# Two DMA rings, two halves of the rows: a row-wise roll with a narrower SBUF part

## The chip, the cores and the metric

The kernel runs on one core of one Trainium2 chip. A core has compute engines (TensorE, VectorE or DVE, ScalarE or ACT, GpSimd or POOL), a sequencer without arithmetic (SyncE or SP), and 16 DMA engines that move data between HBM and HBM, or between HBM and the on-chip memory SBUF. SP, ACT and POOL can issue DMAs, each into a queue of its own. The metric is device time in microseconds (us), lower is better.

## The reference

```python
def setup_inputs():
    return {
        "x": np.random.randn(8192, 8192).astype(np.float32),
        "shift": 100,
    }

def reference(x: np.ndarray, shift: int) -> np.ndarray:
    return np.roll(x, shift, axis=1)
```

Each row of 8192 floats (32 KB) is rotated to the right by 100 columns: output columns 100 to 8191 are input columns 0 to 8091, and output columns 0 to 99 are the last 100 of the input. Nothing is computed; 268.4 MB are read and 268.4 MB are written. The source and destination of one byte lie 400 B apart within a row, except for the 100 columns that wrap around.

## The kernel before

The shift `s` is 100. The kernel cuts each output row at a column `a`, which is `s` rounded up to a multiple of 128, and, by L21 and L22, 128 more: `a` is 256. `g = a - s` is 156.

**Columns `a` to the end** are copied from HBM to HBM by the two hardware queues ("rings"), SP's and ACT's. The rows are taken in blocks of 64 (`c`). Within a block, DMA `j` (0 to 3) has 16 rows, 4e + j for e from 0 to 15, which go one to each DMA engine; each is a contiguous run of 7936 floats (31,744 B). SP issues j = 0 and 2, ACT issues j = 1 and 3, of every block (L36 to L38). So each ring has 256 DMAs of 496 KB, both rings walk through the same blocks from row 0 to row 8191, and an engine's four rows of a block are neighbours in memory. Each queue issues in order, and from its fifth DMA on it waits for an older one to land before it issues another.

**Columns 0 to `a`** go through SBUF on POOL's queue, whose descriptors are written by software ("q0" in the profile). The rows are taken in `n_st` = 4 groups of P x J x Q = 128 x 4 x 4. For three of every four rows, one "lead" DMA reads a contiguous run of `a` floats that begins `s` floats before the row, and so takes in the end of the row above (L66 to L68, 12 DMAs into tile `t`). The run's first `s` floats belong to the output row above, and the rest to the row itself: two copies on VectorE put them into tile `h` (L70 and L73). The end of the fourth row and the beginning of the first are loaded straight into `h` (L69 and L72, 4 DMAs each). When all groups have been loaded, 16 DMAs write `h` to the output (L77), 1 KB to a row. The framework adds the semaphore waits between these; POOL's DMAs cycle through 8 semaphores, so that one is issued when the one eight before it has landed.

All three queues start at once and share the 16 DMA engines.

Of the kernel before, what the change touches and what calls it, by code (L numbers as in the profile page):

```python
# [1 line left out]

# [4 lines left out]


@with_exitstack
def kernel(  # L10
    ctx: ExitStack,
    tc: tile.TileContext,
    x: bass.AP,
    shift: int,
    out: bass.AP,
):
    nc = tc.nc
    n_rows, n_cols = x.shape
    s = shift % n_cols
    a = -(-s // 128) * 128  # L20
    if 0 < a <= 384 and a + 128 <= n_cols:  # L21
        a += 128  # L22
    g = a - s
    P = nc.NUM_PARTITIONS
    engines = [nc.sync, nc.scalar]
    n_chunks = 16
    rows = n_rows // n_chunks

    xm = x.rearrange("(c e j) w -> c j e w", e=16, j=4)
    om = out.rearrange("(c e j) w -> c j e w", e=16, j=4)
    if a < n_cols:
        for c in range(n_rows // 64):  # L36
            for j in range(4):
                engines[j % 2].dma_start(out=om[c, j, :, a:], in_=xm[c, j, :, g:n_cols - s])  # L38
    if a == 0:
        return  # L40


    if a > 512:
        for i in range(n_chunks):
            r = slice(i * rows, (i + 1) * rows)
            nc.gpsimd.dma_start(out=out[r, :s], in_=x[r, n_cols - s:])
            if g > 0:
                nc.gpsimd.dma_start(out=out[r, s:a], in_=x[r, :g])
        return

    Q, J = 4, 4
    n_st = n_rows // (P * Q * J)
    reads = ctx.enter_context(tc.tile_pool(name="reads", bufs=n_st))
    heads = ctx.enter_context(tc.tile_pool(name="heads", bufs=n_st))
    xt = x.rearrange("(k p j q) c -> k q p j c", q=Q, j=J, p=P)
    ot = out.rearrange("(k p j q) c -> k q p j c", q=Q, j=J, p=P)  # L60
    tiles = []
    for k in range(n_st):
        t = reads.tile([P, Q - 1, J, a], x.dtype)
        h = heads.tile([P, Q, J, a], x.dtype)
        for q in range(1, Q):
            lead = bass.AP(tensor=x.tensor, offset=(k * P * J * Q + q) * n_cols - s,  # L66
                           ap=[[J * Q * n_cols, P], [Q * n_cols, J], [1, a]])
            nc.gpsimd.dma_start(out=t[:, q - 1], in_=lead)  # L68
        nc.gpsimd.dma_start(out=h[:, Q - 1, :, :s], in_=xt[k, Q - 1, :, :, n_cols - s:])  # L69
        nc.vector.tensor_copy(h[:, :Q - 1, :, :s], t[:, :, :, :s])  # L70
        if g > 0:
            nc.gpsimd.dma_start(out=h[:, 0, :, s:], in_=xt[k, 0, :, :, :g])  # L72
            nc.vector.tensor_copy(h[:, 1:, :, s:], t[:, :, :, s:])  # L73
        tiles.append(h)
    for k, h in enumerate(tiles):
        for q in range(Q):
            nc.gpsimd.dma_start(out=ot[k, q, :, :, :a], in_=h[:, q])  # L77


# [1 line left out]
_INS = ['x', 'shift']  # L81
_OUTS = [((8192, 8192), 'float32')]

_NUMBERS = {'shift': 100}


# [26 lines left out]
```

## Time and profile before

| what | value |
|---|---|
| median of 6 runs | 819.53 us (819.27 to 821.43) |
| the profiled execution | 821.43 us, its span 819.3 us |
| busy: VectorE, POOL | 7.7 us, 28.8 us |
| DMA packets | 21,060, 276.89 MB, mean 338 GB/s |
| ring copies, issue to landing | 12.6 us (median, SP and ACT alike) |
| POOL's stores, issue to landing | 113.2 us (median) |
| POOL's last issue | 373.4 us after the span's start |

The span is the part of the execution that the profile covers. "GB/s" counts each transfer once, whether it reads HBM and writes HBM, or has SBUF at one end. A queue's share is the time that its packets were open on the 16 engines, as a part of 16 times the span; a packet that waits for memory is open too. q1 and q10 are the two rings, q0 is POOL's queue. Where a queue waits, the row names the waiting queue and line first, and then what it waited for.

### The profile page before, as it was taken

To read this page: it belongs to the slowest core of one execution; us is meant where nothing else is said; L and a number is where in the kernel's file an instruction comes from. 1 tells how busy PE (TensorE), PEld (TensorE's weight loads), DVE (VectorE), ACT (ScalarE), POOL (GpSimd) and SP (SyncE) were. 2 spreads that over 40 slices of the span, in tenths; PEclk is the share of its full clock that TensorE was granted. 3 is DMA by queue.
4 is the path that set the end of the run, shared out by engine and by line. 5 is a ranking of instruction groups with operands and counts; after the bars stand their busy time and mean duration, and the time that the engine had idled before them with its cause. 6 is when DMAs were issued, how large, how long until landed. Compare 5 with 4: busy or idle time off the path is not lost. (4 is left out here: it accounts for less than half of the span.)

```text
span 819.3 us, 617 instructions
## 1 busy us (share of the span) xinstructions
DVE 7.7 (1%) x8; POOL 28.8 (4%) x40
## 2 busy tenths in 40 slices
DVE  0000000000000000000000000000000000000000
POOL 3000000000010000000000000000000000000000
DMA  9999999999999999999999999999999999999997
GB/s 309 336 346 345 346 342 351 348 348 353 352 359 359 353 347 353 350 356 358 336 344 336 336 330 330 336 332 329 335 330 333 331 332 332 336 332 324 327 330 257
DMA packets 21060, 276.89 MB, mean 338 GB/s; under 512 B 8768, under 2 KB 8768, under 8 KB 12864
## 3 DMA queue, kind: packets, MB, share of 16 engines
q10 hardware_dynamic: 8192, 130.04, 46.2%
q1 hardware_dynamic: 8192, 130.04, 45.9%
q0 software_dynamic: 4672, 16.78, 6.9%
q14 instruction: 4, 0.03, 0.0%
HBM read 268.44 MB, written 268.44 MB: 655 GB/s over the span
## 5 line engine op out<-in xcount | busy, mean ns | idle before, releaser
L77 POOL DMA_DIRECT2D out_dram<-h x16 | 13.2, 825 | 198.6 <-DMA out_dram<-h 111.1
L68 POOL DMA_DIRECT2D t<-in_x_dram x12 | 9.5, 793 | 59.8 <-DMA h<-in_x_dram 30.2
L70 DVE COPY h<-t 128x1200 f32<-128x1200 f32 x4 | 3.1, 786 | 233.3 <-DMA t<-in_x_dram 233.3
L73 DVE COPY h<-t 128x1872 f32<-128x1872 f32 x4 | 4.9, 1225 | 0.0
L69 POOL DMA_DIRECT2D h<-in_x_dram x4 | 3.0, 748 | 44.8 <-DMA t<-in_x_dram 44.8
L72 POOL DMA_DIRECT2D h<-in_x_dram x4 | 3.0, 748 | 41.9 <-DMA t<-in_x_dram 41.9
L94 POOL MEMSET const-float32-0.0<- 128x1 f32 x1 | 0.1, 98 | 0.2 <-issue 0.2
L94 POOL MEMSET const-bfloat16-1.0<- 128x1 bf16 x1 | 0.1, 101 | 0.0
L94 POOL MEMSET const-float32-1.0<- 128x1 f32 x1 | 0.1, 98 | 0.0
L94 POOL MEMSET const-uint8-127<- 128x1 uint8 x1 | 0.1, 98 | 0.0
## 6 DMA issues: line engine op xcount, KB each, us to landing
out_dram<-in_x_dram SPq DMA_DIRECT2D x256, 496.0 KB, 12.6
out_dram<-in_x_dram ACTq DMA_DIRECT2D x256, 496.0 KB, 12.6
out_dram<-h POOLq DMA_DIRECT2D x16, 512.0 KB, 113.2
t<-in_x_dram POOLq DMA_DIRECT2D x12, 512.0 KB, 95.0
h<-in_x_dram POOLq DMA_DIRECT2D x4, 312.0 KB, 93.6
h<-in_x_dram POOLq DMA_DIRECT2D x4, 200.0 KB, 98.0
```

The source lines that it names most:

```text
L68: nc.gpsimd.dma_start(out=t[:, q - 1], in_=lead)
L69: nc.gpsimd.dma_start(out=h[:, Q - 1, :, :s], in_=xt[k, Q - 1, :, :, n_cols - s:])
L70: nc.vector.tensor_copy(h[:, :Q - 1, :, :s], t[:, :, :, :s])
L72: nc.gpsimd.dma_start(out=h[:, 0, :, s:], in_=xt[k, 0, :, :, :g])
L73: nc.vector.tensor_copy(h[:, 1:, :, s:], t[:, :, :, s:])
L77: nc.gpsimd.dma_start(out=ot[k, q, :, :, :a], in_=h[:, q])
L94: nc = _bacc.Bacc("TRN2", target_bir_lowering=False, num_devices=1)
```

## The change

`a` loses the extra 128 columns: it is 128, and `g` is 28. The rings' rows are 8064 floats (32,256 B). SP takes the blocks of the first half of the rows and ACT those of the second half, each of them all four `j` of a block; they are issued alternately in the program. `J` is 8, so that POOL's part has two groups of 128 x 8 x 4 rows: 6 lead DMAs and 2 + 2 straight loads, 4 copies, and 8 stores, with 512 B to a row.

```diff
     s = shift % n_cols
     a = -(-s // 128) * 128
-    if 0 < a <= 384 and a + 128 <= n_cols:
-        a += 128
     g = a - s
...
     if a < n_cols:
-        for c in range(n_rows // 64):
+        half = n_rows // 64 // 2
+        for c in range(half):
             for j in range(4):
-                engines[j % 2].dma_start(out=om[c, j, :, a:], in_=xm[c, j, :, g:n_cols - s])
+                for q, eng in enumerate(engines):
+                    eng.dma_start(out=om[q * half + c, j, :, a:], in_=xm[q * half + c, j, :, g:n_cols - s])
...
-    Q, J = 4, 4
+    Q, J = 4, 8
     n_st = n_rows // (P * Q * J)
```

## The prediction

> **What bounds the kernel now.** I read the page's slices and queues first, then the queue's own waits, then the DMA view of two stretches, one with and one without the GpSimd queue's traffic. Compute engines can be left at once: VectorE is busy 7.7 us and POOL 28.8 us of 819.3.
>
> The slices and the queues of the page:
>
> ```profile
> DMA  9999999999999999999999999999999999999997
> GB/s 309 336 346 345 346 342 351 348 348 353 352 359 359 353 347 353 350 356 358 336 344 336 336 330 330 336 332 329 335 330 333 331 332 332 336 332 324 327 330 257
> ...
> q10 hardware_dynamic: 8192, 130.04, 46.2%
> q1 hardware_dynamic: 8192, 130.04, 45.9%
> q0 software_dynamic: 4672, 16.78, 6.9%
> ...
> HBM read 268.44 MB, written 268.44 MB: 655 GB/s over the span
> ```
>
> The 16 DMA engines are busy from the first slice to the last (46.2 + 45.9 + 6.9 = 99.0% of their span). There is no gap to close: the time changes only if the engines have less to do or do it at another rate. The GB/s row, which counts each transfer once, falls from about 350 to about 331 in the middle, where the GpSimd queue (q0) runs dry. The two rings are not short of issues, as the waits of SP's queue show (who waited, for what, us in total, times, longest):
>
> ```profile
> SPq L38 <- DMA out_dram<-in_x_dram: 672.0, 252, 4.3
> ```
>
> 252 of SP's 256 issues stood ready and waited for an older transfer. Now the DMA view of 20 to 180 us, where q0 mostly loads, and then of 500 to 800 us, where it is empty (packets, MB, share of the 16 engines):
>
> ```profile
> q10 hardware_dynamic: 1553, 24.76, 43.1%
> q1 hardware_dynamic: 1546, 24.54, 41.3%
> q0 software_dynamic: 1706, 6.03, 16.1%
> ```
>
> ```profile
> q10 hardware_dynamic: 3129, 49.65, 50.1%
> q1 hardware_dynamic: 3130, 49.69, 49.4%
> ```
>
> What limits the engines is read from two rates. Per engine, the rings move 49.30 MB / (84.4% x 16 x 160 us) = 22.8 GB/s in the first stretch and 99.34 MB / (99.5% x 16 x 300 us) = 20.8 GB/s in the second: a row of 31,744 B takes 1,391 ns beside q0, and 1,526 ns without it. An engine doing a fixed job per byte would not change by 10%. HBM traffic does stay put: a ring's byte is read from HBM and written to it, a q0 byte touches HBM once, so the first stretch has (2 x 49.30 + 6.03) / 160 us = 654 GB/s and the second 2 x 99.34 / 300 us = 662. The same sum gives 659 for 180 to 260 us, 665 for 260 to 400 (mostly q0 stores) and 665 for 400 to 500. So HBM traffic is within 2% of constant while the engines' own rate moves by 10%: I read the bound as HBM, not the engines' count of bytes. (That every slice is 9 tells only that an engine always has a packet open, also one that waits for memory.)
>
> The page "HBM Reference", section Specifications, of the Trainium skill gives a domain about 716 GB/s; 536.9 MB at that would take 750 us by an estimate from that figure, so this run would stand at 91% of it, and a new order would have more to lose than to gain.
>
> **The change part by part.** The profiled execution took 821.43 us with a span of 819.3, 2.1 us outside it; the median of the runs is 819.53, 1.9 below the profiled one. I make the sum on the span and carry the difference over unchanged.
>
> *1. Narrower SBUF part (the two removed lines at L21; a is 128, not 256, and g 28, not 156).* HBM traffic is unchanged: each byte of x is read once and each of out written once, 536.9 MB, by either route. What moves is 8192 x 512 B = 4.19 MB from "load and store through q0" to "one ring copy": q0 falls from 16.78 to 8.39 MB, the rings rise from 260.08 to 264.27 MB, engine bytes in all fall from 276.86 to 272.66 MB. A ring row grows from 31,744 to 32,256 B, in the same 256 DMAs of 16 rows on SP and 256 on ACT.
> - HBM rate held: the stretches with q0 get half as long. Against 662 GB/s, 20 to 180 us lost 160 x 8/662 = 1.9 us, 180 to 260 lost 80 x 3/662 = 0.4, and 260 to 500 gained 240 x 3/662 = 1.1. Net 1.2 lost, half of it returned: about -0.6 us.
> - Durations of each stretch kept for ring bytes (22.8, 22.5, 21.6, 21.0 and 20.8 GB/s per engine from the five stretches named above): with the q0 stretches halved, the rings need 751 us of engine time where they needed 726, q0 27 where it needed 54, in the 780 us from 20 to 800: -2 us.
> - Lower end, flat per byte: 272.66/276.86 of the span, -12.4 us. Only if every engine byte cost the same, which the 10% above contradicts.
> - Upper end, q0 priced by the piece: there are as many contiguous pieces as before (loads 6,144 + 2,048 + 2,048, stores 8,192), only shorter. If they kept q0's whole 6.9% (56.5 us per engine), the added 4.19 MB on the rings at 333 GB/s would come on top: +12.6 us. Single packet records speak against it: in the first 170 us a load packet of four 1,024 B pieces took 281 ns on the mean (1,200 packets) and one of eleven 400 B pieces 343 ns (78 packets), 70 and 31 ns a piece. The packet's bytes set the price, and 8 x 512 B makes the same 4 KB packet.
>
> I take -0.7 us: the first of these, a tenth towards the second, because the HBM rate is the steadiest number of the trace.
>
> *2. J 8 instead of 4 (L55).* Two groups of rows instead of four. The program as built issues 18 DMAs on POOL, not 36, each of 1,024 pieces and up to 512 KB as before, and 4 copies on VectorE, not 8. The rows of before:
>
> ```profile
> L77 POOL DMA_DIRECT2D out_dram<-h x16 | 13.2, 825 | 198.6 <-DMA out_dram<-h 111.1
> L68 POOL DMA_DIRECT2D t<-in_x_dram x12 | 9.5, 793 | 59.8 <-DMA h<-in_x_dram 30.2
> L70 DVE COPY h<-t 128x1200 f32<-128x1200 f32 x4 | 3.1, 786 | 233.3 <-DMA t<-in_x_dram 233.3
> L73 DVE COPY h<-t 128x1872 f32<-128x1872 f32 x4 | 4.9, 1225 | 0.0
> ```
>
> Copies become 2,400 and 672 elements a partition, about 1.5 and 0.5 us each by these rows; POOL's issue time lies between half of 28.8 us (a price per DMA) and all of it (per piece). Neither is on the path: POOL's last issue is at 373 us and its last landing about 113 us later, 330 us before the end. Half the bytes bring that to some 250 us. Cost nothing; it would matter only if q0 outlived the rings. The first copy waits for a larger first group, and only the group's own stores wait behind it.
>
> *3. Halves (L35 to L38).* SP walks rows 0 to 4095, ACT rows 4096 to 8191, in the same blocks of 64 rows, one row per engine. Before, an engine took rows 4e, 4e+1, 4e+2, 4e+3 in turn from the two rings, 32 KB apart; now it alternates between two streams 128 MB apart, each going 32 KB a step. DMA count, rows per DMA, issue time (510 ns on SP, 517 on ACT, under 672 us of waiting) and each ring's bytes stay equal, so both still end together. What stands open is only how HBM takes two distant streams for one. No row shows this. The nearest are the slices that hold ring copies alone (500 us on, the last left out): they run from 324 to 336 GB/s about a mean of 331, with one program at different places of the tensors. That bounds it at +2.2% (+18 us) and -1.5% (-12 us). I take 0: the rate of slices 25 to 36 shows no trend as the rings walk through the second half of both tensors, and within a DMA the 16 rows stand to each other as before.
>
> A rule speaks against this part. The page "DMA: Bandwidth & Descriptors", section Latency and other measured facts, of the Trainium skill, row on HBM row pitch at large powers of two, has copies at a pitch of 512 KiB at 207 GB/s per direction, 2 MiB at 164, and 4 MiB at 103. If two streams a power of two apart collided so, ring time would grow by 207/164, an estimate of some 1,030 us; no run here shows it, and 16 rows 128 KB apart run at 331 here. As a sign it points to slower.
>
> Sum: 819.3 - 0.7 + 0 + 0 = 818.6 us of span, 820.7 for that execution, 818.8 against the median.
>
> **The rivals.** About 0.2% (1.6 us) is what a measurement of this kernel can tell from no change.
> - *A, no change:* HBM stays the bound at the same rate. 818.8, own range 816.5 to 820.5.
> - *B, slower: the two streams cost HBM time.* Place: each ring packet after q0 is done. Price: between 0.3% and the 2.2% of the slowest slice, so 821.3 to 837, middle 827. It decides when a ring row of 32,256 B takes over 1,526 x 32,256/31,744 x 1.003 = 1,555 ns in the q0-free stretch. For it: HBM is the bound, so any lost efficiency shows in full, over all 780 us, and two neighbouring rows become two distant ones. Against it: the rows inside each DMA keep their spacing.
> - *C, faster: engine bytes pay, or separate regions suit HBM.* -2 us by the durations, -12.4 flat: 807 to 817.5, middle 813. For it: the engines are at 99% and get 1.5% fewer bytes. Against it: the HBM sum.
> - *D, slower: 512 B pieces cost as much as 1 KB ones.* Up to +12.6: 821.5 to 832. Against it: the packet records.
> - *The change does not do what it says:* excluded for the transfers' shapes, since the built program has 256 DMAs of 16 x 8064 on each ring; if the rings drifted apart their regions would be as distant anyway.
>
> **How the numbers follow.** A 0.42, B 0.35, C 0.17, D 0.06. A is the likeliest single case and gives the predicted time. Of A, 0.10 falls under -0.2%, 0.28 within, 0.04 above. Faster 0.10 + 0.17 = 0.27; same 0.28; slower 0.04 + 0.35 + 0.06 = 0.45. Range 806 to 837: the lower end is the -12 of parts 1 and 3, not both at once, the upper the +18 of B; what is left out is gains that add up and the rule's large price, under 0.15 together.
>
> **What will show it.** Right: q0 at about 8.4 MB and 3.5 to 4% with its packets ending near 250 us; rings at 132.1 MB each and some 95.5% together; 331 GB/s in the q0-free slices, which begin earlier; an HBM rate of 654 to 656 over the span. B shows as q0-free slices under 330 GB/s with all slices still 9. C shows as those slices above 333. D shows as a q0 share near 6.9% at half the bytes. The prediction falls if q0-free slices move by more than 1%, whatever q0 does: then part 3 was mispriced at 0.

## The result and the profile after

The changed kernel takes 826.07 us (median of 20 runs, 822.11 to 828.87); the kernel before took 820.36 us (median of 42) beside it. The ratio is 1.0069, 95% interval 1.0059 to 1.0080: about 5.7 us slower. The profiled execution has a span of 823.9 us, 4.6 more than before.

The page of the kernel after, slices and queues:

```profile
DMA  9999999999999999999999999999999999999997
GB/s 312 337 340 341 337 347 344 352 356 346 336 347 326 329 332 327 330 327 334 329 334 324 337 324 335 324 324 332 323 337 330 330 321 330 337 327 326 327 326 262
...
q10 hardware_dynamic: 8192, 132.14, 47.8%
q1 hardware_dynamic: 8192, 132.14, 47.2%
q0 software_dynamic: 2336, 8.39, 3.9%
...
HBM read 268.44 MB, written 268.44 MB: 652 GB/s over the span
```

All slices but the last are still 9, so the engines nearly always have a packet open; q0's bytes have halved and its share nearly so; the drop in the GB/s row comes at slice 13 instead of slice 20. After the drop the row lies about 329, not 331. The queue's waits, and the DMA view of 500 to 800 us, in which the rings run alone in both kernels:

```profile
SPq L39 <- DMA out_dram<-in_x_dram: 676.7, 252, 3.5
```

```profile
q1 hardware_dynamic: 3061, 49.49, 50.2%
q10 hardware_dynamic: 3057, 49.16, 49.6%
```

This is 98.65 MB in 300 us where before had 99.34, so HBM traffic of 658 GB/s instead of 662: -0.7%, about the size of the whole loss. Each row leaves two packets in the records, its 32,256 B and one of 4 B, so these are 3,059 rows, and a row takes 99.8% x 16 x 300 us / 3,059 = 1,566 ns (before, a row of 31,744 B took 1,526 ns). The stretch from 20 to 180 us, with q0 beside the rings, lost less: 652 against 654 GB/s (2 x 49.36 + 5.62 MB in 160 us).

POOL and VectorE did what the prediction's part 2 said, and they are done early: q0's last packet ends 253 us after the span's start, of 823.9.

```profile
L78 POOL DMA_DIRECT2D out_dram<-h x8 | 6.9, 954 | 90.6 <-DMA h<-in_x_dram 79.7
L69 POOL DMA_DIRECT2D t<-in_x_dram x6 | 5.4, 910 | 0.8 <-PEq L109 0.8
L71 DVE COPY h<-t 128x2400 f32<-128x2400 f32 x2 | 2.8, 1410 | 115.0 <-DMA t<-in_x_dram 115.0
...
L74 DVE COPY h<-t 128x672 f32<-128x672 f32 x2 | 1.0, 503 | 0.0
```

### The profile page after: what moved, and what is told of

The parts are those of the page before. It is cut to its first block, busy times and chain, and to the rows that moved or that the text cites. A ratio compares the mean times of both kernels' runs of the same rounds, so it can differ in the third digit from the quotient of the medians.

```text
span 823.9 us, 589 instructions
## 1 busy us (share of the span) xinstructions
DVE 3.7 (0%) x4; POOL 16.1 (2%) x22
## 3 DMA queue, kind: packets, MB, share of 16 engines
q0 software_dynamic: 2336, 8.39, 3.9%
## 5 line engine op out<-in xcount | busy, mean ns | idle before, releaser
L78 POOL DMA_DIRECT2D out_dram<-h x8 | 6.9, 954 | 90.6 <-DMA h<-in_x_dram 79.7
L69 POOL DMA_DIRECT2D t<-in_x_dram x6 | 5.4, 910 | 0.8 <-PEq L109 0.8
L71 DVE COPY h<-t 128x2400 f32<-128x2400 f32 x2 | 2.8, 1410 | 115.0 <-DMA t<-in_x_dram 115.0
L70 POOL DMA_DIRECT2D h<-in_x_dram x2 | 1.8, 883 | 15.1 <-DMA t<-in_x_dram 15.1
L73 POOL DMA_DIRECT2D h<-in_x_dram x2 | 1.8, 883 | 14.4 <-DMA t<-in_x_dram 14.4
```

## The experiments

The kernel before took 820 us in some of the groups of runs below and 829 in others, and both values were seen on one chip. So every ratio is against the kernel before of the same group, with its 95% interval, and ratios of different groups are compared only where the difference is well beyond the intervals. That the difference between groups takes all kernels of a group along is supported by e2, e3 and e4 (within 0.12% of a kernel before at 829 us) and by e9 and e10 (within 0.12% of one at 820 us). But all orders except those of the two main kernels were run in one group only, so a ratio that stands alone is weaker evidence than its interval says. The profile's views do not name the DMA engine of a packet; that row e of a DMA goes to engine e, and that an engine takes rows from the two rings in turn, is assumed below, as it was in the prediction.

### Which part costs (before 828.88 us)

*e1, halves alone* (a stays 256, J stays 4):

```diff
-        for c in range(n_rows // 64):
+        half = n_rows // 64 // 2
+        for c in range(half):
             for j in range(4):
-                engines[j % 2].dma_start(out=om[c, j, :, a:], in_=xm[c, j, :, g:n_cols - s])
+                for q, eng in enumerate(engines):
+                    eng.dma_start(out=om[q * half + c, j, :, a:], in_=xm[q * half + c, j, :, g:n_cols - s])
```

> The kernel before with one part of the change: SP takes the first half of the rows and ACT the second, a stays 256 and J stays 4. Theory H (two distant streams cost HBM time): the whole loss is here, about 825.5 us against 820 for the kernel before, and the stretch from 500 to 800 us, ring copies alone, runs at about 329 GB/s instead of 331. Theory W (the narrower SBUF part with its longer ring rows costs it): no change, 819 to 821 us and 331 GB/s in that stretch. Half of the loss, about 823, would say that both cost.

Measured: 831.12 us, 1.0030 (1.0016 to 1.0045).

*e2, the narrow part alone* (the kernel after with the loop of before put back):

```diff
-        half = n_rows // 64 // 2
-        for c in range(half):
+        for c in range(n_rows // 64):
             for j in range(4):
-                for q, eng in enumerate(engines):
-                    eng.dma_start(out=om[q * half + c, j, :, a:], in_=xm[q * half + c, j, :, g:n_cols - s])
+                engines[j % 2].dma_start(out=om[c, j, :, a:], in_=xm[c, j, :, g:n_cols - s])
```

> The kernel after without the halves: a is 128 and J is 8, but both rings walk the same blocks as before. Theory H: 819 to 820 us, my own prediction for this part (0.7 us less than before), with 331 GB/s from 500 to 800 us. Theory W: about 826 us, as the whole change, with 329 GB/s in that stretch.

Measured: 828.70 us, 0.9994 (0.9980 to 1.0007).

*e3, J alone:*

```diff
-    Q, J = 4, 4
+    Q, J = 4, 8
```

> The kernel before with J = 8 alone: two groups of rows, 1 KB pieces, 1 MB per DMA on POOL's queue. All theories: no change, 819 to 821 us, since POOL's queue is done some 300 us before the end. If this run were slower than that, the group size would be part of the loss.

Measured: 827.75 us, 0.9988 (0.9974 to 1.0002).

*e4, a wider SBUF part:*

```diff
     if 0 < a <= 384 and a + 128 <= n_cols:
-        a += 128
+        a += 256
```

> The kernel before with a = 384: ring rows of 31,232 B that start 1,536 B into the output row, which is a multiple of 512 B and not of 1 KB, as in the kernel after (512 B) and unlike before (1,024 B). The SBUF part grows by half, to 25.2 MB, so its queue ends near 700 us. Theory W by alignment (a ring row that starts off a 1 KB boundary is slower): where ring copies run alone, HBM traffic falls from 662 to about 658 GB/s here too, and the time is 3 to 5 us above that of before. Theory W by amount (each 128 columns taken off the rings save time): 5 us below that of before. Theory H: no change, 819 to 821 us.

Measured: 828.45 us, 0.9998 (0.9984 to 1.0011).

The page of e4:

```profile
DMA packets 22596, 281.09 MB, mean 340 GB/s; under 512 B 8768, under 2 KB 8768, under 8 KB 14400
```

The width of the SBUF part does not matter here: 128, 256 and 384 columns take the same time, whether the ring rows start on a multiple of 1 KB or not. Engine bytes go from 272.7 MB (128 columns) to 281 MB (384), and nothing follows from it, which is what a bound by HBM predicts. The loss belongs to the halves. The rates of 500 to 800 us, where the rings run alone, agree in order but not with the numbers expected (331 and 329): e1 first, then e2, by stretches (the last number is GB/s).

```profile
500.00:800.00 300.00, 0.00 (x0) 0.00 (x0) 1.00 1.00 327
500.00:800.00 300.00, 0.00 (x0) 0.00 (x0) 1.00 1.00 329
```

e2 stands at the 329 that was to speak for theory W, but it is no slower than the kernel before of its group, of which there is no profile. Its time decides, not that rate. With 256 columns the loss is 0.30%, less than half of the 0.69% of the whole change's first group; the whole change costs 0.43% in its last group (e18), and from that 0.30% is not clear.

### Distance, neighbours or address bits (before 829.03 us)

Three ideas on why halves cost: the distance of the two streams (D); that an engine's next row is no longer the neighbour of the last (N); that an engine's successive rows agree in their low address bits (L). *e5* is the changed kernel again.

> The changed kernel itself, beside the three below. Halves alone cost 0.30% (0.16 to 0.45), the narrower part alone nothing (-0.06%), and both together 0.69% in another run. If the parts add up and the chip sets the difference, about 1.003 here; if the halves cost more beside longer ring rows, about 1.007.

Measured: 834.40 us, 1.0068 (1.0045 to 1.0092). Of the two outcomes expected, this is the one in which the halves cost more beside the longer ring rows; e18, further down, lies between the two.

*e6, ACT one row ahead:*

```diff
                 for q, eng in enumerate(engines):
-                    eng.dma_start(out=om[q * half + c, j, :, a:], in_=xm[q * half + c, j, :, g:n_cols - s])
+                    i = (j + q) % 4
+                    eng.dma_start(out=om[q * half + c, i, :, a:], in_=xm[q * half + c, i, :, g:n_cols - s])
```

> The changed kernel with ACT one row ahead in its block: SP takes rows 4e + j, ACT rows 4e + (j + 1) mod 4 of the distant block, so that the two streams are 128 MB and 32 KB apart, not 128 MB. Theory L (streams whose addresses agree in their low 21 bits meet in the same part of HBM): the loss goes, 1.000. Theory D (two distant regions) and theory N (an engine's next row is no longer the neighbouring one): no change against the changed kernel.

Measured: 833.65 us, 1.0056 (1.0033 to 1.0078). Theory L expected 1.000 and missed. From here on it was kept in a narrower form, in which what counts is agreement of rows that follow each other on an engine.

*e7, even and odd blocks:* both streams are close together, 2 MB apart.

```diff
-                    eng.dma_start(out=om[q * half + c, j, :, a:], in_=xm[q * half + c, j, :, g:n_cols - s])
+                    eng.dma_start(out=om[2 * c + q, j, :, a:], in_=xm[2 * c + q, j, :, g:n_cols - s])
```

> The changed kernel with SP on the even blocks of 64 rows and ACT on the odd ones: the two streams are 2 MB apart instead of 128 MB, with the same row of the block in both, so the low 21 bits agree as in halves. Theory D: the loss goes, 1.000. Theories L and N: the loss stays, as in the changed kernel.

Measured: 835.45 us, 1.0080 (1.0058 to 1.0103). Theory D falls: 2 MB apart costs as much as 128 MB.

*e8, sixteen regions* (from e2: both rings in the same blocks, only the engines' spacing changed):

```diff
-    xm = x.rearrange("(c e j) w -> c j e w", e=16, j=4)
-    om = out.rearrange("(c e j) w -> c j e w", e=16, j=4)
+    xm = x.rearrange("(e c j) w -> c j e w", e=16, j=4)
+    om = out.rearrange("(e c j) w -> c j e w", e=16, j=4)
```

> The changed kernel's narrow part with both rings in the same blocks again, but a block is now made of 16 groups of 4 rows that lie 512 rows (16 MB) apart, one group per DMA engine: 16 distant streams, while an engine's four rows are still neighbours. Theory D: a multiple of the loss of the two halves, 1.5% or more above before. Theory L in its strong form (all 16 engines agree in their low 24 bits): far more, some 20 to 100%, the order of the rule on row pitch. Theory N: no loss, 1.000, since neighbours stay together.

Measured: 2135 us (median; 1833 to 2322 in 6 runs), 2.2 to 2.8 times as long. The page of e8, of an execution of 2237 us:

```profile
DMA packets 18724, 272.70 MB, mean 122 GB/s; under 512 B 8480, under 2 KB 8480, under 8 KB 10528
## 3 DMA queue, kind: packets, MB, share of 16 engines
q10 hardware_dynamic: 8192, 132.14, 54.9%
q1 hardware_dynamic: 8192, 132.14, 43.0%
q0 software_dynamic: 2336, 8.39, 1.3%
...
HBM read 268.44 MB, written 268.44 MB: 240 GB/s over the span
```

As many packets and bytes as in the kernel after, packets open for 99.2% of the engines' time, and 240 GB/s of HBM traffic instead of some 650. Sixteen streams 16 MB apart are a different matter from sixteen streams 128 KB apart. Theory N, which expected no loss, does not explain this, and the loss is above the 20 to 100% of theory L's strong form; distance and agreement of the addresses are not told apart here. That the halves lose by the same cause in a small measure is not shown.

### What cures it (before 820.18 us)

*e9, ACT two rows ahead:* as e6, with

```diff
-                    i = (j + q) % 4
+                    i = (j + 2 * q) % 4
```

> The changed kernel with ACT two rows ahead in its block: SP takes rows 4e + j, ACT rows 4e + (j + 2) mod 4 of the distant block. An engine's sequence of row numbers within a block is 0, 2, 1, 3, 2, 0, 3, 1, so that no two packets in a row agree in their low 21 address bits (with j + 1 every second pair did: ACT's row j + 1, then SP's row j + 1). Theory L (such pairs meet): the loss goes, 1.000. Theory N (an engine's next row is no longer the neighbouring one): the loss stays, 1.006.

Measured: 820.20 us, 0.9998 (0.9984 to 1.0012). The two halves, 128 MB apart, at no loss, as theory L in its narrower form expected. The changed kernel was not run in this group; halves without the shift were, as ring copies alone (e12).

*e10, no neighbours* (from e2):

```diff
-                engines[j % 2].dma_start(out=om[c, j, :, a:], in_=xm[c, j, :, g:n_cols - s])
+                i = j // 2 + 2 * (j % 2)
+                engines[j % 2].dma_start(out=om[c, i, :, a:], in_=xm[c, i, :, g:n_cols - s])
```

> The narrow part with both rings in the same blocks (the kernel that stood at 0.9994), but SP takes rows 0 and 1 of an engine's four and ACT rows 2 and 3, so that an engine moves rows 0, 2, 1, 3: never a neighbour next, all within the same 128 KB. Theory N: the loss appears, 1.006. Theory L, and any theory by the distance of the streams or by the size of the region in flight: 1.000.

Measured: 819.24 us, 0.9988 (0.9971 to 1.0005). Theory N falls.

*e11 and e12, ring copies alone,* same blocks (from e2) and halves (from the kernel after). In both:

```diff
-    if a == 0:
+    if a < n_cols:
         return
```

> Left out: the first 128 columns of every output row, and all of POOL's and VectorE's work with them. Ring copies alone, both rings in the same blocks, 264.2 MB. At 331 GB/s and 13 us of start and end it takes about 805 to 812 us on this chip. It is the base for the next run.

> Left out: the same as in the run before. Ring copies alone, SP in the first half of the rows and ACT in the second. If the loss sits in the stretch where the rings run alone and q0 covers it elsewhere (0.30% with the rings alone for 40% of the time, 0.69% with them alone for 67%), it is about 1.0% above the run before, some 8 us. If it is spread over the whole time, 0.7%; if it comes from the two rings beside q0, nothing.

Measured: 805.13 us (803.63 to 805.99, 4 runs) and 812.69 us (811.96 to 813.94, 6 runs), so halves cost 812.69 / 805.13 = 0.94%, 7.6 us, and the two sets of runs do not touch. The DMA views of 300 to 780 us, e11 first, then e12:

```profile
DMA packets 9850, 158.90 MB, mean 331 GB/s; under 512 B 4923, under 2 KB 4923, under 8 KB 4923
```

```profile
DMA packets 9727, 156.96 MB, mean 327 GB/s; under 512 B 4860, under 2 KB 4860, under 8 KB 4860
```

With no copy through SBUF and no work on VectorE in it, the same copies in another order run 1.2% slower in this stretch. The cost is in the ring copies themselves. It would also fit e1: the rings run alone for some 41% of e1's time (q0's last packet ends at 490 us) and 69% of the kernel after's (at 253 us); 0.94% of these is 0.4% and 0.6%, beside 0.30% and 0.69% measured. That q0's traffic covers the cost is argued from these four numbers, not shown, and with the 0.43% of e18 in place of 0.69% there is little to explain.

### Does agreement of the addresses explain it (before 820.07 us)

Up to here theory L was alive: rows that agree in their low 21 bits (equal modulo 2 MB) follow each other in e5, e6 and e7 and not in e9 and e10.

*e13, ACT's blocks 32 rows later:*

```diff
+    m = n_rows // 2
+    xs = x[m + 32:n_rows - 32].rearrange("(c e j) w -> c j e w", e=16, j=4)
+    os = out[m + 32:n_rows - 32].rearrange("(c e j) w -> c j e w", e=16, j=4)
...
-                for q, eng in enumerate(engines):
-                    eng.dma_start(out=om[q * half + c, j, :, a:], in_=xm[q * half + c, j, :, g:n_cols - s])
+                nc.sync.dma_start(out=om[c, j, :, a:], in_=xm[c, j, :, g:n_cols - s])
+                if c < half - 1:
+                    nc.scalar.dma_start(out=os[c, j, :, a:], in_=xs[c, j, :, g:n_cols - s])
+                else:
+                    r = (m if j < 2 else n_rows - 32) + j % 2
+                    nc.scalar.dma_start(out=out[r:r + 31:2, a:], in_=x[r:r + 31:2, g:n_cols - s])
```

> The changed kernel with ACT's blocks begun 32 rows later (its first and last 32 rows go in four DMAs of 16 rows at the end), so that an engine's two rows are 128 MB and 1 MB apart. The 16 engines together still have the same rows modulo 2 MB in flight in both rings; only which engine has which differs. Theory L1 (agreeing rows collide where one follows the other on the same engine): the loss goes, 1.000. Theory L2 (they collide wherever they are in flight in the two rings): the loss stays, 1.006 to 1.007.

Measured: 818.45 us, 0.9980 (0.9967 to 0.9993). L2 falls, L1 stands. (Neither in this group nor with e9 was the changed kernel itself run; its 0.43 to 0.69% come from three other groups.)

*e14, loops exchanged:*

```diff
-        for c in range(half):
-            for j in range(4):
+        for j in range(4):
+            for c in range(half):
```

> The changed kernel with its two loops exchanged, j outside and c inside: now every row that an engine takes agrees with the one before it in the low 21 bits (steps of 128 MB, then 2 MB less), where in the changed kernel every second one did. Theories L1 and L2 with a price per pair: twice the loss, about 1.014. If it is the agreement of the two rings and not that of consecutive rows that counts: unchanged, 1.007.

Measured: 818.19 us, 0.9977 (0.9965 to 0.9989). Every row now agrees with the one before it, and the kernel is not twice as bad but faster than the kernel before. L1 falls too. In the views by stretches, the row of 500 to 800 us, e14 first, then the kernel after:

```profile
500.00:800.00 300.00, 0.00 (x0) 0.00 (x0) 1.00 1.00 334
500.00:800.00 300.00, 0.00 (x0) 0.00 (x0) 1.00 1.00 329
```

*e15 and e16, the engines' spacing* (from e2): 256 KB and 64 KB instead of 128 KB. For e15 (e16 has 2 for 8 and 32 for 128):

```diff
-    xm = x.rearrange("(c e j) w -> c j e w", e=16, j=4)
-    om = out.rearrange("(c e j) w -> c j e w", e=16, j=4)
+    xm = x.rearrange("(c e j) w -> c j e w", e=16, j=8)
+    om = out.rearrange("(c e j) w -> c j e w", e=16, j=8)
     if a < n_cols:
-        for c in range(n_rows // 64):
-            for j in range(4):
+        for c in range(n_rows // 128):
+            for j in range(8):
```

> The narrow part with both rings in the same blocks (0.9994), but blocks of 128 rows: each engine has 8 neighbouring rows, the engines stand 256 KB apart, and a DMA covers 4 MB. If address bit 21 (2 MB) no longer tells parts of HBM apart, engines e and e + 8 now agree in their low 21 bits, and the time rises clearly, by several per cent up to tens. If that bit still counts: 1.000.

> The same with blocks of 32 rows: 2 neighbouring rows per engine, the engines 64 KB apart, a DMA within 1 MB. All rows of four blocks in flight differ in their low 21 bits only by half as much as before. If the bits from 16 on are worth the same, 1.000. A gain would say that the spacing of 128 KB already costs something; a loss that the low bits of that spacing tell less apart.

Measured: e15 828.22 us, 1.0100 (1.0072 to 1.0129); e16 818.15 us, 0.9981 (0.9968 to 0.9994). With both rings in the same blocks and no halves, blocks of 128 rows cost at least about as much as the halves did, and blocks of 32 rows cost nothing. The edit changes two things at once, the engines' spacing and the number of rows that an engine has in a block.

### The second slow order, and the cure tried on it (before 828.77 us)

*e17* (from e15): the rings set apart within an engine's eight rows.

```diff
-                engines[j % 2].dma_start(out=om[c, j, :, a:], in_=xm[c, j, :, g:n_cols - s])
+                i = j // 2 + 4 * (j % 2)
+                engines[j % 2].dma_start(out=om[c, i, :, a:], in_=xm[c, i, :, g:n_cols - s])
```

> The 256 KB spacing (8 neighbouring rows per engine, both rings in the same blocks, 1.010), with SP taking rows 0 to 3 of an engine's eight and ACT rows 4 to 7, so that the rings are 128 KB apart instead of 32 KB. Theory M (two rings that go slowly through the same few rows hold too like rows at one time; setting them apart by a bit from 64 KB to 1 MB cures it, as the 2 rows and the 32 rows did for the halves): 0.998 to 1.001. Theory P (the spacing of the 16 engines, 256 KB, is what costs, whatever the rings do): 1.010 as before.

> The changed kernel once more, beside the run above. It stood at 1.0069 and 1.0068 where the kernel before took 820 and 829 us. If the pattern of the two halves is the cause whatever the chip, 1.007 again; if it depends on where the tensors lie, it can differ.

Measured: e17 830.27 us, 1.0016 (1.0002 to 1.0029); e18, the changed kernel, 832.59 us, 1.0043 (1.0026 to 1.0061). By the ratios theory P falls: the spacing is as in e15, and most of its loss is gone. But e15 was not run beside e17. In time itself e17 is not faster (830.27 against 828.22 us), and both move 328 GB/s from 500 to 800 us; the gain rests on the kernel before being at 829 us here and at 820 us there. Theory M has the direction right, with 1.0016 just above its range and its interval reaching into it. The changed kernel is slower in all three groups that had it, by 0.4 to 0.7%; 1.0043 is lower than the 1.0069 of the first, their intervals just overlap, and whether the size depends on where the tensors lie stays open.

What stays open is the rule behind it. Shown is that the cost sits in the ring copies, that it depends on the order in which the two rings take their rows (e9, e13 and e14 have the halves without the cost), and that neither distance, nor the neighbour, nor agreement modulo 2 MB predicts it. No run changed where `x` and `out` lie in HBM, so a collision of reads with writes is a rival that was not tested. One description fits the orders tried, e8 aside: those are slow in which an engine stays for eight rows in the same blocks with the two rings at most one row apart there, the last row counted as next to the first (e1, e5, e6, e7, e12, e15), and those are not in which it moves on to other blocks after two or four rows (the kernel before, e2, e10, e11, e14, e16) or in which the rings are set apart by 2, 4 or 32 rows (e9, e13, and e17 nearly). It was made after the fact, and no run was left to test it on an order of its own.

## Why the prediction was wrong

The forecast was 818.8 us and no change; measured was +0.69%, inside the range of 806 to 837 and on the slow side of the 0.2%. The likeliest single case was A, and rival B happened. The chances leaned better than the number: added up over the cases they gave 0.45 to slower and 0.28 to no change.

- **The step that failed is part 3, "I take 0".** The term "how HBM takes two distant streams for one" measured +7.6 us for ring copies alone (e12 against e11) and +5.7 us in the whole kernel, well inside the bound of -12 to +18 that the part itself had set. Both reasons for 0 were beside the matter: a flat rate over the second half of the tensors says something of places, not of two rings together, and "the 16 rows stand to each other as before" leaves out how the two rings' rows follow each other, and with other orders the loss was gone (e9, e13, e14). Why that order costs HBM time stays open.
- **B's price and place were right, its name was not.** B ran from 821.3 to 837 with its middle at 827, and decided at 1,555 ns for a ring row; the profile has 1,566 ns, and 329 GB/s where B was to show under 330. But B was called the cost of two distant streams. Two streams 128 MB apart are free in e9, and two 2 MB apart cost in e7. The prediction's own sign for a mispriced part 3, q0-free slices that move by more than 1%, was too coarse: they moved by 0.7%, and the whole kernel lost 0.69%.
- **The bound was read rightly.** The same HBM traffic takes the same time with 128, 256 and 384 columns (e2, e4), and engine bytes are worth nothing that can be seen: C's "-12.4 flat" and D's "+12.6" are both out. Parts 1 and 2 together, at -0.7 us, stand against 0.9994 (0.9980 to 1.0007) in e2, -0.5 us with an uncertainty of 1 us; no change at all lies within that too, C's -2 us just outside.
- **Part 2 was right.** J costs nothing (e3, 0.9988 with 1 in its interval), the copies took 1,410 and 503 ns beside the 1.5 and 0.5 us forecast, POOL's busy time 16.1 us, near the half. q0 had 8.39 MB, 3.9% and its last packet at 253 us, for 8.4 MB, 3.5 to 4% and 250.
- **The rule that spoke against the change was set aside too lightly, and would have been misused if taken whole.** The page "DMA: Bandwidth & Descriptors", section Latency and other measured facts, of the Trainium skill has the loss with row pitches of 2 MiB and more. Here 16 rows of a DMA 16 MB apart fell from about 331 to 122 GB/s (e8), which goes the same way; at 256 KB, below its table, the cost was 1.0% in one order (e15) and 0.16% in another (e17). Two rings, not 16 streams, paid 0.4 to 0.7%, not the 26% of the estimate. That estimate put the pitch between the two rings; in these runs the large loss came with the pitch between the 16 rows of a DMA.

## What to carry to other kernels

When a copy is held by HBM and no engine is idle, its order in memory is a term of its own: price it by a run, not at zero, and look at which rows all queues and engines hold at one time, not only at each DMA's shape. Keep the 16 rows of a DMA close together in memory (64 to 128 KB apart here; 16 MB cost a factor of 2.2 to 2.8), and if two queues walk separate regions, try them out of step: here 2 and 32 rows went without loss and 1 row did not. Changing which route the bytes take (SBUF or HBM to HBM) moved nothing here, where HBM traffic stayed the same.

## What was not expected

- Exchanging two loops (e14, c inside j) makes the halves 0.23% faster than the kernel before, and 32 rows of offset (e13) 0.20%; a spacing of 64 KB (e16) does the same for the common blocks. All three beat the kernel before, by little: their intervals end at 0.9989 to 0.9994. All three also have 128 columns and J = 8, and e2 and e10, which have these and the common blocks, stand at 0.9994 and 0.9988, so how much of the gain is the order's is not shown.
- A step of 16 MB between the rows of a DMA costs 1,000 to 1,500 us with the number of packets and their bytes unchanged.
- The kernel before took 820 us in three groups of runs and 829 in three others. What the runs of a group share to make that difference isn't known.
